# Attention scores of two heads issued together on alternating row halves, and a gating stage with 512-column mixing matmuls

## Chip, core and metric

One core of a Trainium2 chip runs one launch. The metric is the device time of that launch in microseconds (us). The kernel before takes 1171.48 us (median of three runs, 1170.75 to 1171.59).

## What is computed

The reference runs two layers on a (256, 2048) fp32 activation. Layer 0 normalises the rows, projects to queries, keys, values and gates, runs two banded attention mixers of 16 heads of width 64 each, gates both with SiLU, projects back and adds the residual. Layer 1 normalises, projects to u, v and a gate, and mixes v over positions:

```python
s = einsum('bgrnqd,bgnkd->bgrnqk', qb, kb) + bias[:, :, None]   # scores, both mixers
p = exp(s - m[..., None]);  u = einsum('bgrnqk,bgnkd->bgrnqd', p, vb)
...
v = _rms(v, v_g).reshape(Bn, S // 128, 128, 16, 256)            # layer 1
ws = w_s * tril(ones)                                           # 16 groups of 128x128
s = einsum('gts,bnsgc->bntgc', ws, v) + b_s.T[:, :, None]
y = u * s.reshape(Bn, S, 4096) * gate;  return x + y @ w_out
```

So a head has a 128 x 256 score block (the second 128 queries against all 256 keys) and a 128 x 128 block (the first 128 queries), and layer 1 mixes 256 columns of v per group, once per chunk n of 128 positions (two chunks).

## The kernel before, in words

**Projections.** `gemm` (lines 100 to 126) makes a 256 x 512 output block from weights that stream in through SP's DMA queue. `wtile` (lines 75 to 88) splits each 256 x 512 weight tile into a rounded part `whi` (ScalarE, line 85) and a rest `wlo` (VectorE, line 86), and three fp32r matmuls of 512 columns each (lines 121 to 123) add up the product. There are 44 such calls with 512 columns (the last block of the last one is cut into halves) and one with 256.

**Fillers.** After every second bank-and-k step, that is after six matmuls of 512 columns, `gemm` calls `fill()` (line 92), which advances the oldest generator of a list by one `yield`. Attention, gating, transposes and splits are such generators; so their instructions are written between the matmuls of the next projection. The tile framework then orders each engine's instructions by this order and by its own estimate of when operands and buffers are free, so that neighbours can change places.

**Attention** (lines 275 to 368) is called four times with eight heads. Step i of the loop (line 359) issues `scores(i)`, `ptrans(i-3)` and `pv(i-5)`, then yields; the `tiny`, `sb`, `pr` and `pt` tiles come from pools (`mid`: 10 buffers for `sb`, `pr`, `pt`). `scores(i)` (line 282) takes one of two "s" PSUM banks and issues, on row half i % 2 (partitions 0 to 63 or 64 to 127, where the 64 values of the head lie), three fp32r matmuls of 256 columns (lines 296 to 298) and one fp32 matmul of 128 columns (line 299), which the engine runs as two. VectorE adds the bias and takes maxima (lines 302, 305, 310 or 313), ScalarE the exponentials (lines 315, 317). `ptrans` (line 321) transposes the three 128 x 128 blocks into the one "t" bank and ScalarE copies them out (line 327); `pv` (line 332) multiplies them by v, 64 columns each (lines 339 to 341, two passes each).

**Gating** (lines 547 to 604). `ws` holds the masked mixing matrices. `sgu(c)`, eight times, scales the two matrices of its groups by the row norm of v on GpSimd (`wsn`, line 577), once per chunk n, splits them (`wsh` line 579, `wsl` line 580), splits v (`vh` line 582, `vl` line 583), and issues, per chunk and group, three matmuls of 256 columns (lines 589 to 591), then adds the bias and multiplies by u on VectorE (line 594). After that it waits for the gate, multiplies on GpSimd (line 601) and transposes (line 377). The row norm `rsv` (line 567) is known after the last of eight v projections.

Of the kernel before, what the change touches and what calls it, by code (L numbers as in the profile page):

```python
# [10 lines left out]
F32 = mybir.dt.float32  # L11
# [22 lines left out]
def trunk(ctx, tc, x, xT, ev_g, w_in0, w_kva, qk_g, sinks, w_out0, od_g, w_in1, v_g, w_sT, b_s,  # L34
# [2 lines left out]

    cons = ctx.enter_context(tc.tile_pool(name="cons", bufs=1))
    wpool = ctx.enter_context(tc.tile_pool(name="wpool", bufs=4))
    big = ctx.enter_context(tc.tile_pool(name="big", bufs=26))  # L40
    mid = ctx.enter_context(tc.tile_pool(name="mid", bufs=10))
    tiny = ctx.enter_context(tc.tile_pool(name="tiny", bufs=4))
    ps = ctx.enter_context(tc.tile_pool(name="ps", bufs=4, space=bass.MemoryType.PSUM))

# [12 lines left out]
    def psum(tag, bufs):  # L57
        return ps.tile([P, 512], F32, tag=tag, bufs=bufs, name=nm(tag))
# [216 lines left out]
    def attention(mix, h0, first_bias, qTb, kTb, vfn, ydst):  # L275

        (q0, q1), (k0, kh, kl) = qTb, kTb
        bts = [first_bias, None]
        st = {}
        grp = {}  # L280

        def scores(i):
            h = h0 + i
            if i % 4 == 0:
                bt = bts[i // 4]
                nmx = tiny.tile([P, 4, 2], F32, tag="nmx", name=nm("nmx"))
                mx = tiny.tile([P, 4, 2], F32, tag="mx", name=nm("mx"))
                l = tiny.tile([P, 4, 2], F32, tag="l", name=nm("l"))
                grp[i // 4] = (bt, mx, nmx, l)
            bt, mx, nmx, l = grp[i // 4]  # L290
            j = i % 4
            half = slice((i % 2) * 64, (i % 2) * 64 + 64)
            sp = psum("s", 2)
            kp = h // 8 if mix == 0 else i // 2
            qh, ql = q1[half, 0, i // 2, :], q1[half, 1, i // 2, :]
            nc.tensor.matmul(sp[:, 0:256], qh, kh[half, kp, :], start=True, stop=False)  # L296
            nc.tensor.matmul(sp[:, 0:256], qh, kl[half, kp, :], start=False, stop=False)
            nc.tensor.matmul(sp[:, 0:256], ql, kh[half, kp, :], start=False, stop=True)
            nc.tensor.matmul(sp[:, 256:384], q0[half, i // 2, :], k0[half, kp, :],  # L299
                             start=True, stop=True)  # L300
            sb = m2([P, 384], nm("sb"))
            nc.vector.tensor_tensor_reduce(out=sb[:, 0:256], in0=sp[:, 0:256], in1=bt[:, j, :],  # L302
                                           scale=1.0, scalar=NEG, op0=ALU.add, op1=ALU.max,
                                           accum_out=mx[:, j, 1:2])
            nc.vector.tensor_tensor_reduce(out=sb[:, 256:384], in0=sp[:, 256:384],
                                           in1=bt[:, j, P:2 * P],
                                           scale=1.0, scalar=NEG, op0=ALU.add, op1=ALU.max,
                                           accum_out=mx[:, j, 0:1])
            if mix == 0:
                nc.vector.tensor_scalar(nmx[:, j, :], mx[:, j, :], snk[:, h:h + 1], -1.0,  # L310
                                        op0=ALU.max, op1=ALU.mult)
            else:
                nc.vector.tensor_scalar(nmx[:, j, :], mx[:, j, :], -1.0, None, op0=ALU.mult)  # L313
            pr = m2([P, 384], nm("pr"))
            nc.scalar.activation(pr[:, 0:256], sb[:, 0:256], AF.Exp, bias=nmx[:, j, 1:2],  # L315
                                 accum_out=l[:, j, 1:2])
            nc.scalar.activation(pr[:, 256:384], sb[:, 256:384], AF.Exp, bias=nmx[:, j, 0:1],
                                 accum_out=l[:, j, 0:1])
            st[i] = pr

        def ptrans(i):
            pr = st[i]
            tp = psum("t", 1)
            for b in range(3):
                nc.tensor.transpose(tp[:, b * P:(b + 1) * P], pr[:, b * P:(b + 1) * P], ident)  # L325
            pt = m2([P, 384], nm("pt"))
            nc.scalar.copy(pt, tp[:, 0:384])
            st[i] = pt

        ub = {}  # L330

        def pv(i):
            pt = st.pop(i)
            if i % 4 == 0:
                ub[0] = psum("u", 1)
            up = ub[0].rearrange("p (t h d) -> p t h d", t=2, d=DH)
            j = i % 4
            v0, v1 = vfn(i)
            nc.tensor.matmul(up[:, 0, j, :], pt[:, 256:384], v0, start=True, stop=True)  # L339
            nc.tensor.matmul(up[:, 1, j, :], pt[:, 0:128], v0, start=True, stop=False)  # L340
            nc.tensor.matmul(up[:, 1, j, :], pt[:, 128:256], v1, start=False, stop=True)  # L341
            if j == 3:
                _, mx, nmx, l = grp[i // 4]
                if mix == 0:
                    es = tiny.tile([P, 4, 2], F32, tag="es", name=nm("es"))
                    hh = h0 + i - 3
                    nc.vector.tensor_tensor(es, nmx,
                                            snk[:, hh:hh + 4].unsqueeze(2).broadcast_to([P, 4, 2]),
                                            op=ALU.add)
                    nc.scalar.activation(es, es, AF.Exp)  # L350
                    nc.vector.tensor_tensor(l, l, es, op=ALU.add)
                r = tiny.tile([P, 4, 2], F32, tag="rl", name=nm("rl"))
                nc.vector.reciprocal(r, l)
                yv = ydst.rearrange("p t (h d) -> p t h d", d=DH)[:, :, i - 3:i + 1, :]
                nc.vector.tensor_tensor(yv, up,
                                        r.rearrange("p h t -> p t h").unsqueeze(3)
                                        .broadcast_to([P, 2, 4, DH]), op=ALU.mult)

        for i in range(8 + L2):
            if i < 8:  # L360
                scores(i)
            if L1 <= i < 8 + L1:
                ptrans(i - L1)
            if i >= L2:
                pv(i - L2)
            if i == 0:
                bts[1] = bias_tile(mix, h0 + 4)
            yield

    def split_T(y, yT, q, tags):  # L370
# [173 lines left out]
    nc.scalar.dma_start(trit, tri)  # L544
    bst = cons.tile([P, 16], F32, name="bst")
    nc.scalar.dma_start(bst, b_s)
    ws = []
    for j in range(2):
        t = c4([P, 8, P], nm("ws"))
        nc.gpsimd.dma_start(t, w_sT[j].rearrange("s (g t) -> s g t", g=8))  # L550
        nc.gpsimd.tensor_tensor(t, t, trit.unsqueeze(1).broadcast_to([P, 8, P]), op=ALU.mult)
        ws.append(t)

    in1 = lambda c: gemm(yTk(hT1), KT, w_in1[c], 512)
    ssv = cons.tile([P, 2, 8], F32, name="ssv")
# [14 lines left out]

    def sgu(c, u, gate):
        y = c4([P, 2, 512], nm("y"))
        wsn = m2([P, 2, 2, P], nm("wsn"))
        wsh = mid.tile([P, 2, 2, P], F32R, tag="m2", name=nm("wsh"))
        wsl = mid.tile([P, 2, 2, P], F32R, tag="m2", name=nm("wsl"))
        for n in range(2):
            nc.gpsimd.tensor_scalar(wsn[:, n], ws[c // 4][:, (2 * c) % 8:(2 * c) % 8 + 2, :],  # L577
                                    rsv[:, n:n + 1], None, op0=ALU.mult)
        nc.scalar.copy(wsh, wsn)
        nc.vector.tensor_tensor(wsl, wsn, wsh.bitcast(F32), op=ALU.subtract)  # L580
        vh, vl = c4([P, 2, 512], nm("vh"), F32R), c4([P, 2, 512], nm("vl"), F32R)
        nc.scalar.copy(vh, vt[c])  # L582
        nc.vector.tensor_tensor(vl, vt[c], vh.bitcast(F32), op=ALU.subtract)  # L583
        yield
        for n in range(2):
            sp = psum("s", 2)
            for gi in range(2):
                cs = slice(gi * 256, (gi + 1) * 256)
                nc.tensor.matmul(sp[:, cs], wsh[:, n, gi, :], vh[:, n, cs], start=True, stop=False)
                nc.tensor.matmul(sp[:, cs], wsh[:, n, gi, :], vl[:, n, cs], start=False, stop=False)  # L590
                nc.tensor.matmul(sp[:, cs], wsl[:, n, gi, :], vh[:, n, cs], start=False, stop=True)  # L591
            for gi in range(2):
                cs = slice(gi * 256, (gi + 1) * 256)
                nc.vector.scalar_tensor_tensor(y[:, n, cs], sp[:, cs],
                                               bst[:, 2 * c + gi:2 * c + gi + 1], u[:, n, cs],
                                               op0=ALU.add, op1=ALU.mult)
            yield
        while gate[0] is None:
            yield
        yield  # L600
        nc.gpsimd.tensor_tensor(y, y, gate[0], op=ALU.mult)  # L601
        yield
        yield
        yield from split_T(y, yT1, c, [("t", 1), ("u", 1)])
# [85 lines left out]
```

## Time and profile before

| what | value |
| --- | --- |
| median of three runs | 1171.48 us (1170.75 to 1171.59) |
| profiled execution, its own time | 1171.01 us |
| its span, first to last instruction of the program | 1169.2 us |
| TensorE matmuls (PE) | 1162.0 us busy, 99% of the span |
| TensorE weight loads (PEld) | 963.0 us, 82% |
| VectorE (DVE) / ScalarE (ACT) / GpSimd (POOL) | 55% / 51% / 12% |

The profiled time lies 1.8 us above its span, and 0.5 us under the median. A matmul's busy time includes the latency of the array and overlaps the next one's, so what a matmul costs in a stream is read from the distance of the starts, not from its duration.

### The profile page before, as it was taken

What the parts mean: (1) busy time and instruction counts of PE and PEld (TensorE: products, weight loads), DVE (VectorE), ACT (ScalarE), POOL (GpSimd) and SP (SyncE); (2) the same over time, 40 slices, a digit from 0 to 9 for tenths busy, and PEclk for the clock granted to TensorE, in tenths of its full rate; (3) what the DMA queues carried; (4) which work ended last, traced back from release to release, by engine and by line L of the source; (5) the groups of instructions that cost most, each with busy time, mean ns of one, the idle gap of its engine ahead of it and who ended that gap; (6) DMA issues with size and microseconds to landing.
All of it is one profiled execution on the core that took longest, in us unless ns stands there. A gap on an engine that the chain in (4) does not pass through costs nothing.

```text
span 1169.2 us, 14610 instructions
## 1 busy us (share of the span) xinstructions
PE 1162.0 (99%) x5546; PEld 963.0 (82%) x5546; DVE 647.5 (55%) x837; ACT 595.2 (51%) x818; POOL 135.7 (12%) x85
## 2 busy tenths in 40 slices
PE   9999999999999999999999999999999999999998
PEld 7887888788788888888888888888888888888887
DVE  6586556655645555554556555565556555454453
ACT  6556654544654544544545554555464455433332
POOL 0131111112103000211215110100000000000000
PEclk9999999999999999999999999999999999999999
DMA  9675335436436655666665555555555665566661
GB/s 349 232 245 195 127 108 184 172 109 208 160 123 219 196 186 183 203 212 200 202 213 178 184 188 190 181 178 187 186 187 171 190 187 173 198 215 199 200 213 37
DMA packets 63638, 218.37 MB, mean 187 GB/s; under 512 B 7632, under 2 KB 10320, under 8 KB 63312
## 3 DMA queue, kind: packets, MB, share of 16 engines
q1 hardware_dynamic: 60352, 209.74, 55.3%
q0 software_dynamic: 2080, 7.34, 2.0%
q8 instruction: 43, 0.70, 0.2%
q10 hardware_dynamic: 1136, 0.36, 0.1%
q14 instruction: 27, 0.22, 0.1%
HBM read 215.32 MB, written 2.10 MB: 186 GB/s over the span
## 4 chain that ended last, share of the span: by engine, by line
PE 96%; DVE 1%; POOL 1%; ACT 1%; DMA 0%; issue 0%; SPq 0%; ACTq 0%; POOLq 0%
PE g L121 30%; PE g L123 29%; PE g L122 29%; PE t L325 1%; POOL wsn L577 1%; PE s L296 1%; PE t L377 1%; PE s L299 1%; PE u L340 1%; PE u L341 1%; PE t L218 1%; PE u L339 1%; DVE wlo L86 0%; DMA wraw<-in_w_in_dram 0%; ACT whi L85 0%
## 5 line engine op out<-in xcount | busy, mean ns | idle before, releaser
L86 DVE TENSOR_TENSOR wlo<-wraw,whi 128x1024 fp32r<-128x1024 f32 (+1 forms) x393 | 514.0, 1312 | 427.3 <-ACT whi L85 426.5
L85 ACT CAST whi<-wraw 128x1024 fp32r<-128x1024 f32 (+1 forms) x393 | 409.1, 1043 | 480.9 <-PE g L123 457.1
L121 PE MATMUL g<-whi,hTh 128*128 128x512 f32 (+1 forms) x1184 | 464.6, 393 | 0.6 <-ACT whi L85 0.6
L122 PE MATMUL g<-wlo,hTh 128*128 128x512 f32 (+1 forms) x1184 | 458.9, 388 | 0.5 <-DVE wlo L86 0.5
L123 PE MATMUL g<-whi,hTl 128*128 128x512 f32 (+1 forms) x1184 | 459.4, 388 | 0.0
L121 PEld LDWEIGHTS g<-whi,hTh 128*128 128x128 f32 x1184 | 222.4, 188 | 45.2 <-ACT whi L85 1.0
L123 PEld LDWEIGHTS g<-whi,hTl 128*128 128x128 f32 x1184 | 222.5, 188 | 44.7
L122 PEld LDWEIGHTS g<-wlo,hTh 128*128 128x128 f32 x1184 | 222.7, 188 | 42.5 <-DVE wlo L86 1.0
L121 PE MATMUL g<-whi,yTh 128*128 128x512 f32 (+1 forms) x416 | 156.2, 375 | 0.0
L122 PE MATMUL g<-wlo,yTh 128*128 128x512 f32 (+1 forms) x416 | 155.3, 373 | 0.0
L123 PE MATMUL g<-whi,yTl 128*128 128x512 f32 (+1 forms) x416 | 155.2, 373 | 0.0
L123 PEld LDWEIGHTS g<-whi,yTl 128*128 128x128 f32 x416 | 78.3, 188 | 14.1
L122 PEld LDWEIGHTS g<-wlo,yTh 128*128 128x128 f32 x416 | 78.4, 188 | 13.5
L121 PEld LDWEIGHTS g<-whi,yTh 128*128 128x128 f32 x416 | 78.4, 188 | 13.6
L601 POOL TENSOR_TENSOR y<-y,gt 128x1024 f32<-128x1024 f32 x8 | 19.2, 2405 | 265.2 <-ACT gt L191 265.2
L565 POOL TENSOR_TENSOR v<-v,gv 128x1024 f32<-128x1024 f32 x8 | 21.9, 2743 | 220.2 <-ACT junk L562 220.2
L302 DVE CUSTOM_DVE_ANT_0 sb<-s,bias 128x256 f32<-128x256 f32 x32 | 13.5, 422 | 27.7 <-PE s L299 27.7
L577 POOL TENSOR_SCALAR wsn<-ws,rstdv 128x256 f32<-128x256 f32 x16 | 20.3, 1282 | 60.6 <-PE s L591 57.3
L191 ACT ACT_TABLE_LOAD x20 | 25.7, 1283 | 1.0 <-PE g L123 0.7
L315 ACT ACTIVATE pr<-sb,nmx 128x256 f32<-128x256 f32 x32 | 16.3, 510 | 18.9 <-DVE nmx L313 13.6
L272 POOL TENSOR_TENSOR bias<-bias,ba 128x1024 f32<-128x1024 f32 x8 | 20.8, 2598 | 33.9 <-DMA bias<-in_bias_dram 33.9
L583 DVE TENSOR_TENSOR vl<-v,vh 128x1024 fp32r<-128x1024 f32 x8 | 9.8, 1225 | 16.4 <-ACT vh L582 16.4
(130 smaller groups left out, 627.3 us busy)
## 6 DMA issues: line engine op xcount, KB each, us to landing
wraw<-in_w_in_dram SPq DMA_DIRECT2D x287, 512.0 KB, 3.7
wraw<-in_w_out_dram SPq DMA_DIRECT2D x96, 512.0 KB, 3.6
bias<-in_bias_dram POOLq DMA_DIRECT2D x8, 512.0 KB, 3.9
xT<-in_xT_dram SPq DMA_DIRECT2D x8, 256.0 KB, 5.1
xr<-in_x_dram SPq DMA_DIRECT2D x2, 1024.0 KB, 10.9
wraw<-in_w_kva_dram SPq DMA_DIRECT2D x8, 256.0 KB, 3.4
gv<-in_v_g_dram POOLq DMA_DIRECT2D x8, 256.0 KB, 3.1
out_dram<-o SPq DMA_DIRECT2D x7, 256.0 KB, 5.0
```

What stands on the lines that cost most here:

```text
L85: nc.scalar.copy(hi[:, js, :cw], raw[:, js, :cw])
L86: nc.vector.tensor_tensor(lo[:, js, :cw], raw[:, js, :cw], hi[:, js, :cw].bitcast(F32), op=ALU.subtract)
L121: nc.tensor.matmul(o, ah[:, sl], whi[:, k, a:b], start=st, stop=False)
L122: nc.tensor.matmul(o, ah[:, sl], wlo[:, k, a:b], start=False, stop=False)
L123: nc.tensor.matmul(o, al[:, sl], whi[:, k, a:b], start=False, stop=en)
L191: nc.scalar.activation(z[:, tt, :cw], acc[tt][:, :cw], func, scale=rs[:, tt:tt + 1])
L272: nc.gpsimd.tensor_tensor(bt, bt, ba[:, mix:mix + 1, :].broadcast_to([P, 4, 256]), op=ALU.add)
L302: nc.vector.tensor_tensor_reduce(out=sb[:, 0:256], in0=sp[:, 0:256], in1=bt[:, j, :], scale=1.0, scalar=NEG, op0=ALU.add, op1=ALU.max, acc ...
L315: nc.scalar.activation(pr[:, 0:256], sb[:, 0:256], AF.Exp, bias=nmx[:, j, 1:2], accum_out=l[:, j, 1:2])
L565: nc.gpsimd.tensor_tensor(v, v, gv.unsqueeze(1).broadcast_to([P, 2, 512]), op=ALU.mult)
L577: nc.gpsimd.tensor_scalar(wsn[:, n], ws[c // 4][:, (2 * c) % 8:(2 * c) % 8 + 2, :], rsv[:, n:n + 1], None, op0=ALU.mult)
L601: nc.gpsimd.tensor_tensor(y, y, gate[0], op=ALU.mult)
```

## The change

`scores` now takes an even head number and issues two heads at once, into two "s" banks: the three fp32r matmuls in the order first head, second head, first head, and so on, then the two fp32 matmuls. The loop goes in steps of two with two yields each: first the two score blocks, then two `ptrans` and two `pv` after the next yield (14 yields for 13). In the gating stage the masked matrices are split once, ahead of the stage; the row norm goes into the split of v (ScalarE with a scale per row, VectorE multiply and subtract, per chunk); and the mixing matmuls run per group over both chunks, 512 columns each. The buffers are 27 for the large pool (26 before) and 9 for `mid` (10).

```diff
-    big = ctx.enter_context(tc.tile_pool(name="big", bufs=26))
-    mid = ctx.enter_context(tc.tile_pool(name="mid", bufs=10))
+    big = ctx.enter_context(tc.tile_pool(name="big", bufs=27))
+    mid = ctx.enter_context(tc.tile_pool(name="mid", bufs=9))
...
-            sp = psum("s", 2)
-            kp = h // 8 if mix == 0 else i // 2
-            qh, ql = q1[half, 0, i // 2, :], q1[half, 1, i // 2, :]
-            nc.tensor.matmul(sp[:, 0:256], qh, kh[half, kp, :], start=True, stop=False)
-            nc.tensor.matmul(sp[:, 0:256], qh, kl[half, kp, :], start=False, stop=False)
-            nc.tensor.matmul(sp[:, 0:256], ql, kh[half, kp, :], start=False, stop=True)
-            nc.tensor.matmul(sp[:, 256:384], q0[half, i // 2, :], k0[half, kp, :],
-                             start=True, stop=True)
...
+            sps = [psum("s", 2), psum("s", 2)]
+            halves = [slice(0, 64), slice(64, 128)]
+            for qpart, kpart, st_, en_ in ((0, kh, True, False), (0, kl, False, False),
+                                           (1, kh, False, True)):
+                for sp, half in zip(sps, halves):
+                    nc.tensor.matmul(sp[:, 0:256], q1[half, qpart, pq, :], kpart[half, kp, :],
+                                     start=st_, stop=en_)
+            for sp, half in zip(sps, halves):
+                nc.tensor.matmul(sp[:, 256:384], q0[half, pq, :], k0[half, kp, :],
+                                 start=True, stop=True)
+            for i, sp in zip((i0, i0 + 1), sps):
...
-        for i in range(8 + L2):
+        for i in range(0, 8 + L2 + 1, 2):
             if i < 8:
                 scores(i)
-            if L1 <= i < 8 + L1:
-                ptrans(i - L1)
-            if i >= L2:
-                pv(i - L2)
-            if i == 0:
-                bts[1] = bias_tile(mix, h0 + 4)
+                if i == 0:
+                    bts[1] = bias_tile(mix, h0 + 4)
+            yield
+            for k in (i, i + 1):
+                if L1 <= k < 8 + L1:
+                    ptrans(k - L1)
+                if L2 <= k < 8 + L2:
+                    pv(k - L2)
             yield
...
         nc.gpsimd.tensor_tensor(t, t, trit.unsqueeze(1).broadcast_to([P, 8, P]), op=ALU.mult)
-        ws.append(t)
+        wsh, wsl = c4([P, 8, P], nm("wsh"), F32R), c4([P, 8, P], nm("wsl"), F32R)
+        nc.scalar.copy(wsh, t)
+        nc.vector.tensor_tensor(wsl, t, wsh.bitcast(F32), op=ALU.subtract)
+        ws.append((wsh, wsl))
...
         for n in range(2):
-            nc.gpsimd.tensor_scalar(wsn[:, n], ws[c // 4][:, (2 * c) % 8:(2 * c) % 8 + 2, :],
-                                    rsv[:, n:n + 1], None, op0=ALU.mult)
-        nc.scalar.copy(wsh, wsn)
-        nc.vector.tensor_tensor(wsl, wsn, wsh.bitcast(F32), op=ALU.subtract)
-        vh, vl = c4([P, 2, 512], nm("vh"), F32R), c4([P, 2, 512], nm("vl"), F32R)
-        nc.scalar.copy(vh, vt[c])
-        nc.vector.tensor_tensor(vl, vt[c], vh.bitcast(F32), op=ALU.subtract)
+            nc.scalar.activation(vh[:, n, :], vt[c][:, n, :], AF.Copy, scale=rsv[:, n:n + 1])
+            nc.vector.scalar_tensor_tensor(vl[:, n, :], vt[c][:, n, :], rsv[:, n:n + 1],
+                                           vh[:, n, :].bitcast(F32),
+                                           op0=ALU.mult, op1=ALU.subtract)
...
-        for n in range(2):
+        for gi in range(2):
             sp = psum("s", 2)
...
+            nc.tensor.matmul(o, wsh[:, g, :], vh[:, :, cs], start=True, stop=False)
+            nc.tensor.matmul(o, wsh[:, g, :], vl[:, :, cs], start=False, stop=False)
+            nc.tensor.matmul(o, wsl[:, g, :], vh[:, :, cs], start=False, stop=True)
+            nc.vector.scalar_tensor_tensor(y[:, :, cs], o, bst[:, 2 * c + gi:2 * c + gi + 1],
+                                           u[:, :, cs], op0=ALU.add, op1=ALU.mult)
```

## Rows read from the trace of the kernel before

**Rows 1.** The page: busy time by engine, granted clock in 40 slices, the chain.

```profile
PE 1162.0 (99%) x5546; PEld 963.0 (82%) x5546; DVE 647.5 (55%) x837; ACT 595.2 (51%) x818; POOL 135.7 (12%) x85
...
PEclk9999999999999999999999999999999999999999
...
PE 96%; DVE 1%; POOL 1%; ACT 1%; DMA 0%; issue 0%; SPq 0%; ACTq 0%; POOLq 0%
```

**Rows 2.** Timeline, 98.8 to 101.2 us: start, duration (us), engine, line, operation.

```profile
98.92 0.39 PE L122 MATMUL g<-wlo,hTh 128*128 128x512 f32 x1
...
99.15 0.39 PE L123 MATMUL g<-whi,hTl 128*128 128x512 f32 x1
99.46 0.18 PEld L296 LDWEIGHTS s<-kh,q 64*128 64x128 f32 x1 [0.35 <-issue]
99.46 0.38 PE L296 MATMUL s<-kh,q 64*128 64x256 f32 x1
99.57 0.19 PEld L297 LDWEIGHTS s<-kl,q 64*128 64x128 f32 x1
...
99.69 0.28 PE L297 MATMUL s<-kl,q 64*128 64x256 f32 x1
...
99.80 0.28 PE L298 MATMUL s<-kh,q 64*128 64x256 f32 x1
...
99.92 0.38 PE L299 MATMUL s<-k,q 64*128 64x128 f32 x2
...
100.23 0.50 PE L121 MATMUL g<-whi,hTh 128*128 128x512 f32 x1
...
100.57 0.40 PE L122 MATMUL g<-wlo,hTh 128*128 128x512 f32 x1
```

**Rows 3.** By line and form, whole span: busy us, mean ns, idle before, releaser.

```profile
L577 POOL TENSOR_SCALAR wsn<-ws,rstdv 128x256 f32<-128x256 f32 x16 | 20.3, 1282 | 60.6 <-PE s L591 57.3 <-DVE rstdv L184 3.4
...
L327 ACT COPY pt<-t 128x384 f32<-128x384 f32 x32 | 14.9, 467 | 7.7 <-PE t L325 7.7
...
L302 DVE CUSTOM_DVE_ANT_0 sb<-s,bias 128x256 f32<-128x256 f32 x32 | 13.5, 422 | 27.7 <-PE s L299 27.7
...
L296 PE MATMUL s<-kh,q 64*128 64x256 f32 x32 | 12.2, 382 | 0.0
L299 PE MATMUL s<-k,q 64*128 64x128 f32 x64 | 12.2, 270 | 0.0
...
L583 DVE TENSOR_TENSOR vl<-v,vh 128x1024 fp32r<-128x1024 f32 x8 | 9.8, 1225 | 16.4 <-ACT vh L582 16.4
...
L589 PE MATMUL s<-vh,wsh 128*128 128x256 f32 x32 | 8.9, 279 | 0.0
```

**Rows 4.** Timeline of PE, 121 to 134 us: one head's transposes and pv.

```profile
122.89 0.49 PE L325 MATMUL t<-ident,pr 128*128 128x128 f32 x3
...
123.39 0.39 PE L340 MATMUL u<-kva,pt 128*128 128x64 f32 x2
123.61 0.39 PE L341 MATMUL u<-kva,pt 128*128 128x64 f32 x2
123.81 0.48 PE L123 MATMUL g<-whi,hTl 128*128 128x512 f32 x1
```

**Rows 5.** Timeline of PE, 693 to 699 us: mixing matmuls, then projection matmuls.

```profile
694.76 0.28 PE L589 MATMUL s<-vh,wsh 128*128 128x256 f32 x1
...
695.48 0.40 PE L121 MATMUL g<-whi,hTh 128*128 128x512 f32 x1
...
696.41 0.39 PE L122 MATMUL g<-wlo,hTh 128*128 128x512 f32 x1
...
697.77 0.39 PE L122 MATMUL g<-wlo,hTh 128*128 128x512 f32 x1
```

**Rows 6.** Stretches (first attention, gating): busy us of each engine, clock, DMA share.

```profile
99.00:133.00 34.00, 34.00 (x191) 27.23 (x189) 17.29 (x56) 26.18 (x57) 0.00 (x0) 1.00 0.34 105
...
650.00:990.00 340.00, 340.00 (x1567) 282.94 (x1566) 184.71 (x174) 176.55 (x188) 25.07 (x13) 1.00 0.58 184
```

More of the change, by code (lines that the diff above doesn't have):

```diff
@@ L280, in attention, with scores @@
         grp = {}
[L282 to L285, printed above, removed]
+        def scores(i0):
+            if i0 % 4 == 0:
                 nmx = tiny.tile([P, 4, 2], F32, tag="nmx", name=nm("nmx"))
@@ L288, in scores @@
                 l = tiny.tile([P, 4, 2], F32, tag="l", name=nm("l"))
[L289 to L292, printed above, removed]
-            sp = psum("s", 2)
-            kp = h // 8 if mix == 0 else i // 2
-            qh, ql = q1[half, 0, i // 2, :], q1[half, 1, i // 2, :]
-            nc.tensor.matmul(sp[:, 0:256], qh, kh[half, kp, :], start=True, stop=False)
-            nc.tensor.matmul(sp[:, 0:256], qh, kl[half, kp, :], start=False, stop=False)
@@ L298, in scores @@
-            nc.tensor.matmul(sp[:, 0:256], ql, kh[half, kp, :], start=False, stop=True)
-            nc.tensor.matmul(sp[:, 256:384], q0[half, i // 2, :], k0[half, kp, :],
-                             start=True, stop=True)
[L301 to L319, printed above, removed]
+                grp[i0 // 4] = (bts[i0 // 4], mx, nmx, l)
+            bt, mx, nmx, l = grp[i0 // 4]
+            pq = i0 // 2
+            kp = (h0 + i0) // 8 if mix == 0 else pq
@@ new lines, in scores @@
+            for i, sp in zip((i0, i0 + 1), sps):
+                h = h0 + i
+                j = i % 4
+                sb = m2([P, 384], nm("sb"))
+                nc.vector.tensor_tensor_reduce(out=sb[:, 0:256], in0=sp[:, 0:256],
+                                               in1=bt[:, j, :],
+                                               scale=1.0, scalar=NEG, op0=ALU.add, op1=ALU.max,
+                                               accum_out=mx[:, j, 1:2])
+                nc.vector.tensor_tensor_reduce(out=sb[:, 256:384], in0=sp[:, 256:384],
+                                               in1=bt[:, j, P:2 * P],
+                                               scale=1.0, scalar=NEG, op0=ALU.add, op1=ALU.max,
+                                               accum_out=mx[:, j, 0:1])
+                if mix == 0:
+                    nc.vector.tensor_scalar(nmx[:, j, :], mx[:, j, :], snk[:, h:h + 1], -1.0,
+                                            op0=ALU.max, op1=ALU.mult)
+                else:
+                    nc.vector.tensor_scalar(nmx[:, j, :], mx[:, j, :], -1.0, None, op0=ALU.mult)
+                pr = m2([P, 384], nm("pr"))
+                nc.scalar.activation(pr[:, 0:256], sb[:, 0:256], AF.Exp, bias=nmx[:, j, 1:2],
+                                     accum_out=l[:, j, 1:2])
+                nc.scalar.activation(pr[:, 256:384], sb[:, 256:384], AF.Exp,
+                                     bias=nmx[:, j, 0:1], accum_out=l[:, j, 0:1])
+                st[i] = pr
@@ L572, in sgu @@
         y = c4([P, 2, 512], nm("y"))
-        wsn = m2([P, 2, 2, P], nm("wsn"))
-        wsh = mid.tile([P, 2, 2, P], F32R, tag="m2", name=nm("wsh"))
-        wsl = mid.tile([P, 2, 2, P], F32R, tag="m2", name=nm("wsl"))
+        vh, vl = c4([P, 2, 512], nm("vh"), F32R), c4([P, 2, 512], nm("vl"), F32R)
         for n in range(2):
-            nc.gpsimd.tensor_scalar(wsn[:, n], ws[c // 4][:, (2 * c) % 8:(2 * c) % 8 + 2, :],
-                                    rsv[:, n:n + 1], None, op0=ALU.mult)
@@ L584, in sgu @@
+        wsh, wsl = ws[c // 4]
         yield
-        for n in range(2):
+        for gi in range(2):
             sp = psum("s", 2)
[L587 to L596, printed above, removed]
+            o = sp.rearrange("p (n c) -> p n c", n=2)
+            cs = slice(gi * 256, (gi + 1) * 256)
+            g = (2 * c + gi) % 8
+            nc.tensor.matmul(o, wsh[:, g, :], vh[:, :, cs], start=True, stop=False)
[3 more added lines that the diff above has]
+                                           u[:, :, cs], op0=ALU.add, op1=ALU.mult)
```

## Prediction

> **What bounds the kernel now.** I read the page first: matmuls cover 99% of the span, the granted clock is full in every slice (2.4 GHz, the upper of the two levels), and 96% of the chain that ended last is PE [rows 1]. So PE's stream of matmuls is the bound, and a part of the change is worth what it takes out of that stream, or puts in. A matmul's printed duration includes latency, so the stream is read from start to start in a timeline. Next, the timeline around one score burst [rows 2]: projection matmuls of 512 columns follow each other after 0.23 us (98.92 to 99.15). The first score matmul starts 0.31 after the last of them, 0.08 late; its weight load starts with it, not ahead of it, so the next one comes 0.23 later (99.46 to 99.69) instead of about 0.115, which is what the two behind it need (99.69, 99.80, 99.92). The same toll is paid on the way out: 99.92 to 100.23 for two fp32 passes, and 0.34 instead of 0.23 for the first projection matmul behind. There is one such burst per head, 32 in all, with 64 fp32 passes (L296, L299 [rows 3]). In the other stages I looked at the stretches: in the first attention ScalarE is busy 26.18 of 34 us and VectorE 17.29, in the gating stage 176.55 and 184.71 of 340 [rows 6]; both have room, and GpSimd has more.
>
> **Price of a burst.** From L123 at 99.15 to the second projection matmul at 100.57 are 1.42 us; two projection distances (0.46) lie in it anyway, so a burst costs 0.96 [rows 2]. The streaming in it is 3 x 0.115 for the 256-column matmuls and 2 x 0.11 for the fp32 passes, 0.565 (the passes' 0.11 is taken from L340 to L341, 0.22 for two passes [rows 4]). The other 0.395, some 0.40, is the toll for changing from 128 to 64 rows and back.
>
> **Scores, the toll.** 16 bursts of two heads instead of 32 of one: 16 x 0.395 = 6.3 us less. Nothing hides this: it lies in PE's stream.
>
> **Scores, the alternation.** No row of before shows matmuls on different row halves next to each other, because projections stand between any two heads. So its price is bounded from both sides. (a) In turn: each still takes 0.115; a pair costs 0.395 + 2 x 0.565 = 1.53, against 1.92 for two bursts. (b) Side by side: the second head's matmul runs with the first's. The three steps take 3 x 0.115; of the fp32 passes (order: first head twice, then second head twice) only one finds a partner, if matmuls start in program order, so 3 x 0.11. A pair then costs 0.395 + 0.345 + 0.33 = 1.07 and saves 0.85, or 13.6 us for 16. (c) Each change of half pays the entry toll of [rows 2], 0.08 late start and 0.115 exposed weight load: seven changes in a pair, 7 x 0.195 = 1.37 more.
> I take (b). The rows for it: two operands, two row halves and two PSUM banks have nothing in common but the issue; a weight load already runs beside the streaming matmul of its own half (L297's load at 99.57 under L296 [rows 2]), and the toll comes where the shape of the used rows changes, which it does not between halves. The row against it: where matmuls are short, loads pace the stream. 64 columns take as long as 128, two passes in 0.22 [rows 4], so if two halves cannot be loaded at once, (a) holds, because a score matmul then has a load of the same length in front of it.
> The Trainium skill, TensorEngine Tiling (Array Packing), Key Properties, says that different tiles can load weights and multiply in parallel, and that changing the tiling mode, not just the tile, drains the engine. By it (b) holds and the sum is the forecast; by the pacing of loads in rows 4 alone it would be (a), 7 us more. No row here shows the first half of the rule; the toll in rows 2 agrees with the second.
>
> **Transposes and pv in twos.** A head's transposes and pv take 122.89 to 123.81, 0.92 us, whether one follows another or not [rows 4]. New is that the second head's transposes want the single "t" bank again as soon as the first's are copied out: 0.47 us on ScalarE (L327 [rows 3]). In program order a pv of 0.92 - 0.33 = 0.59 us (three transposes of 0.11 subtracted) stands between and covers the copy, unless ScalarE is late; projection matmuls can cover it too. If that cover is gone, 12 such places (three per attention call) cost up to 0.5 each, 6 us. I take 0.5 in all. A few bursts before went straight into transposes and saved part of the exit toll; that is inside this 0.5.
>
> **Softmax for two heads in one burst.** VectorE now gets two score blocks at once; per head its first pass takes 0.42 (L302 [rows 3]) and the whole some 1.1 us. The next pair is due two fills, at least 12 projection matmuls or 2.7 us plus the pair itself, later, so the banks come free in time: cost nothing, up to 1 us a pair if projections' splits delay VectorE. One yield more per call moves pv back one fill; the result of the last call is read a projection later, so nothing waits. One `mid` buffer less holds (nine live at most): the same cover.
>
> **Gating.** Twelve matmuls of 256 columns become six of 512. Six of the former take 694.76 to 695.48, 0.72; six of the latter 696.41 to 697.77, 1.36 [rows 5]. So 1.44 becomes 1.36, eight times: 0.6 us less. GpSimd loses 16 scalings, 20.3 us (L577 [rows 3]), none of which PE waited for; its queue holds the multiplication by the gate behind them, with idle time to spare. ScalarE and VectorE lose eight conversions of 512 columns each and gain two of 1024 each ahead of the stage, at most 1.23 each by L583 [rows 3]; the split of v goes by chunk, with the row norm in it, a few tenths more per call on each engine, beside 340 - 185 us of free VectorE time [rows 6]. At the first call the split waits for the row norm, as the scaled matrices did; a stall of some tenths either way. Two more large tiles stay live with one buffer more; at the last call one half of v's split may have to wait for a projection operand to come free, with a projection of 22 us (96 x 0.23) as cover. No DMA is added or moved; SP's queue is as before. Cost: nothing.
>
> **Sum.** -13.6 + 0.5 - 0.6 = -13.7 us. Against the profiled execution's 1171.0 us that is 1157.3; the median lies 0.5 above that execution, so 1157.8.
>
> **The rivals.**
> *In turn* (a): the halves take turns, since loads pace them. -6.3 + 0.5 - 0.6 = -6.4, so 1165.1. For it: rows 4; against it: separate rows, and the load that already runs beside a matmul.
> *Drain at each change of half* (c), the slower side: 16 x (1.37 - 0.395) = +15.6, with the rest +15.5, so 1187.0. It decides when a change costs more than 0.06 us (0.40 over seven changes): above that the kernel is slower. For it: the toll exists in rows 2; against it: there the number of rows changes, here only their place.
> *The order undone*: the second bank is not free when the framework orders PE's work, so a pair is cut in two with projections between, and the second transposes wait. Then the tolls come back and up to 6 us are added: 1166 to 1177, about 1171. For it: the order follows estimates, and two "s" banks leave no spare; against: the two fills of room above.
>
> **Chances.** Measurement of this kernel tells some 0.2% (2.3 us) from no change. Side by side 0.45, in turn 0.34, drain 0.09, order undone 0.12. The first two are both faster by over 0.2%, and 0.03 of the last: 0.82. Same: 0.06, all of the order undone. Slower: drain 0.09 and 0.03 of the last, 0.12. The range takes in side by side with its unknowns (a fourth fp32 pass hidden as well, -1.8 us, and 1 us of stalls less than taken) and in turn with 2.5 us of its own: 1155.2 to 1167.5.
>
> **What the profile after should show.** Score matmuls of two heads within a few hundredths of each other, then a step of about 0.12, a pair taking 1.07 us beyond two projection distances: side by side. Even steps of 0.115, the pair 1.53: in turn. Steps of 0.2 to 0.3 within a burst: drain. More than 16 bursts, or projections inside one: the order undone. Mixing matmuls 0.23 apart, no `wsn` on GpSimd, and idle PE in front of transposes if the copy is late. The forecast is wrong if the first distance is not there, whatever the tolls do.

## The result, and the profile after

The changed kernel takes 1158.97 us (median of four runs, 1158.16 to 1159.27) against 1171.24 us for the kernel before on the same chip: a ratio of 0.9894, 95% interval 0.9881 to 0.9906, 12.3 us less. The forecast was 1157.8 us, from 1155.2 to 1167.5. In a second set of runs, beside other executions of the kernel before, the ratio was again 0.9894 (0.9877 to 0.9910).

The page of the changed kernel, parts 1, 2 and 4, against [rows 1]:

```profile
span 1157.1 us, 14468 instructions
...
PE 1149.3 (99%) x5498; PEld 952.8 (82%) x5498; DVE 641.3 (55%) x823; ACT 592.7 (51%) x820; POOL 115.5 (10%) x69
...
PEclk9999999999999999999999999999999999999999
...
PE 95%; DVE 1%; ACT 1%; DMA 1%; issue 1%; SPq 0%; ACTq 0%
```

TensorE is still the bound, at full granted clock. There are 48 matmuls fewer, the mixing matmuls of double width, and GpSimd is 20 us less busy. The span fell by 12.1 us.

The timeline of the first burst, with the columns of [rows 2]:

```profile
99.41 0.39 PE L123 MATMUL g<-whi,hTl 128*128 128x512 f32 x1
99.73 0.19 PEld L298 LDWEIGHTS s<-kh,q 64*128 64x128 f32 x2 [0.35 <-issue]
99.73 0.38 PE L298 MATMUL s<-kh,q 64*128 64x256 f32 x2
...
99.95 0.28 PE L298 MATMUL s<-kl,q 64*128 64x256 f32 x2
...
100.07 0.28 PE L298 MATMUL s<-kh,q 64*128 64x256 f32 x2
...
100.19 0.38 PE L301 MATMUL s<-k,q 64*128 64x128 f32 x4
...
100.50 0.50 PE L121 MATMUL g<-whi,hTh 128*128 128x512 f32 x1
...
100.83 0.40 PE L122 MATMUL g<-wlo,hTh 128*128 128x512 f32 x1
```

Each score line now stands for two matmuls (x2), or four passes (x4), and takes no longer than it did for one: two matmuls take 0.38 us from first start to last end, with a step of 0.12 to the next two, and the four fp32 passes take the 0.31 that two took. Weight loads come in pairs too. From L123 at 99.41 to L122 at 100.83 are 1.42 us, exactly the 1.42 of one head in [rows 2]. Two heads for the price of one.

I added up, over all matmuls of the span, the distance from each start to the next start. It gives the stream by kind, before and after: scores 24.8 and 14.4 us, mixing 11.9 and 11.0, the 4512 projection matmuls of 512 columns with what stands behind them 1042.8 and 1041.9, transposes 26.5 and 26.7, pv 19.4 and 19.2. The differences add up to -12.2 us; the span's is -12.1.

Not every burst is clean. Of 16 pairs, 12 cost 0.97 to 0.99 us, priced as in the prediction. Timeline of PE, one that waits for its second bank (103.44), one that was cut in two (from 113.25), one with transposes inside (from 229.64):

```profile
103.44 0.38 PE L298 MATMUL s<-kh,q 64*128 64x256 f32 x1
104.13 0.38 PE L298 MATMUL s<-kh,q 64*128 64x256 f32 x1 [0.30 <-DVE mx L311]
...
113.25 0.38 PE L298 MATMUL s<-kh,q 64*128 64x256 f32 x1
...
114.03 0.50 PE L121 MATMUL g<-whi,hTh 128*128 128x512 f32 x1
114.46 0.38 PE L298 MATMUL s<-kh,q 64*128 64x256 f32 x1
...
229.99 0.28 PE L298 MATMUL s<-kh,q 64*128 64x256 f32 x2
230.28 0.55 PE L331 MATMUL t<-ident,pr 128*128 128x128 f32 x3
230.76 0.49 PE L301 MATMUL s<-k,q 64*128 64x128 f32 x4
```

In the first, the second head's matmul stands 0.69 behind the first head's, until VectorE has emptied its bank (`mx`, line 311). The second has one projection matmul between its heads and pays the toll twice: the two halves cost 1.08 each. A like place to the third is at 309.84; each pays a second toll around its transposes. The breaks in the second and third stand in the program itself, in the order that the framework wrote; the first is a wait on the chip. And there are two new halts ahead of transposes, 1.34 us at 136.0 and 0.79 at 187.3 (counted as the distance of two starts beyond the usual 0.23), where one of 1.20 at 212.9 in the kernel before has shrunk to 0.40. The timeline around the larger:

```profile
133.07 2.40 POOL L400 TENSOR_TENSOR ya<-ya,gt 128x1024 f32<-128x1024 f32 x1 [33.87 <-DVE ya L361]
...
134.09 2.46 DVE L86 TENSOR_TENSOR wlo<-wraw,whi 128x1024 fp32r<-128x1024 f32 x1 [1.14 <-ACT whi L85]
...
136.47 0.47 DVE L231 SCALAR_TENSOR_TENSOR q<-t,gain,q 128x256 fp32r<-128x256 f32 x1
...
137.04 0.47 ACT L234 ACTIVATE q<-t,gain 128x256 f32<-128x256 f32 x1 [2.62 <-DVE q L231]
...
137.57 0.66 PE L218 MATMUL t<-ident,qa 128*128 128x128 f32 x4 [1.18 <-ACT q L234]
```

The transposes of the next queries want the "t" bank; ScalarE's last read of it waits for VectorE's, and that stands behind a split of weights that took 2.46 us, twice the usual. It started while GpSimd multiplied by the gate (133.07 to 135.47) and ended 1.08 us after the product.

### The profile page after: what moved, and what is told of

It reads as the page before. It is cut to its first block, busy times and chain, and to the rows that moved or that the text cites. A ratio compares the mean times of both kernels' runs of the same rounds, so it can differ in the third digit from the quotient of the medians.

```text
span 1157.1 us, 14468 instructions
## 1 busy us (share of the span) xinstructions
PE 1149.3 (99%) x5498; PEld 952.8 (82%) x5498; DVE 641.3 (55%) x823; ACT 592.7 (51%) x820; POOL 115.5 (10%) x69
## 4 chain that ended last, share of the span: by engine, by line
PE 95%; DVE 1%; ACT 1%; DMA 1%; issue 1%; SPq 0%; ACTq 0%
PE g L121 30%; PE g L122 30%; PE g L123 30%; PE t L331 1%; DMA wraw<-in_w_in_dram 1%; ACT whi L85 1%; DVE wlo L86 1%; PE s L298 1%; PE u L347 1%; PE u L346 1%; PE t L385 1%; PE u L345 0%; PE t L218 0%; PE s L599 0%; PE s L600 0%
## 5 line engine op out<-in xcount | busy, mean ns | idle before, releaser
L122 PE MATMUL g<-wlo,hTh 128*128 128x512 f32 (+1 forms) x1184 | 459.5, 388 | 0.6 <-DVE wlo L86 0.6
L123 PE MATMUL g<-whi,hTl 128*128 128x512 f32 (+1 forms) x1184 | 458.9, 388 | 0.0
L123 PEld LDWEIGHTS g<-whi,hTl 128*128 128x128 f32 x1184 | 222.6, 188 | 45.0
L122 PEld LDWEIGHTS g<-wlo,hTh 128*128 128x128 f32 x1184 | 222.8, 188 | 44.0 <-DVE wlo L86 1.4
L122 PE MATMUL g<-wlo,yTh 128*128 128x512 f32 (+1 forms) x416 | 155.3, 373 | 0.0
L123 PE MATMUL g<-whi,yTl 128*128 128x512 f32 (+1 forms) x416 | 155.3, 373 | 0.0
L123 PEld LDWEIGHTS g<-whi,yTl 128*128 128x128 f32 x416 | 78.3, 188 | 14.1
L121 PEld LDWEIGHTS g<-whi,yTh 128*128 128x128 f32 x416 | 78.4, 188 | 13.6
L122 PEld LDWEIGHTS g<-wlo,yTh 128*128 128x128 f32 x416 | 78.4, 189 | 13.5
L608 POOL TENSOR_TENSOR y<-y,gt 128x1024 f32<-128x1024 f32 x8 | 19.2, 2404 | 344.9 <-ACT gt L191 344.9
L577 POOL TENSOR_TENSOR v<-v,gv 128x1024 f32<-128x1024 f32 x8 | 22.1, 2757 | 219.5 <-ACT junk L574 219.5
L333 ACT COPY pt<-t 128x384 f32<-128x384 f32 x32 | 15.0, 469 | 9.8 <-PE t L331 9.8
L588 DVE SCALAR_TENSOR_TENSOR vl<-v,rstdv,vh 128x512 fp32r<-128x512 f32 x16 | 11.3, 749 | 12.4 <-ACT vh L587 12.4
```

What stands on the lines that cost most here:

```text
L121: nc.tensor.matmul(o, ah[:, sl], whi[:, k, a:b], start=st, stop=False)
L122: nc.tensor.matmul(o, ah[:, sl], wlo[:, k, a:b], start=False, stop=False)
L123: nc.tensor.matmul(o, al[:, sl], whi[:, k, a:b], start=False, stop=en)
L577: nc.gpsimd.tensor_tensor(v, v, gv.unsqueeze(1).broadcast_to([P, 2, 512]), op=ALU.mult)
```

## The experiments

Each ratio is to the kernel before, measured with the same set of runs (its medians there: 1172.31, 1172.01 and 1172.36 us for the three sets).

**Both heads on one row half.**

```diff
-            halves = [slice(0, 64), slice(64, 128)]
+            halves = [slice(0, 64), slice(0, 64)]
```

> The changed kernel with both heads of a pair read from row half 0 (so every odd head computes the scores of the even head; that part of the result is another one). Order, banks, counts and tolls stay. Theory (halves run side by side): without the second half a burst costs 0.40 of toll and ten steps of 0.11 to 0.12, 1.53 us instead of 0.97; 16 bursts give +9.0 us, so 1168 us. Rival (the gain comes from halving the bursts and from alternating banks alone): stays at 1159 us, with bursts of 0.97 us.

Measured: 1166.23 us, ratio 0.9947 (0.9932 to 0.9962), so 6.2 us more than the changed kernel by the ratios. Timeline of PE, the first burst:

```profile
99.93 0.50 PE L298 MATMUL s<-kh,q 64*128 64x256 f32 x2
100.27 0.39 PE L298 MATMUL s<-kl,q 64*128 64x256 f32 x2
100.50 0.40 PE L298 MATMUL s<-kh,q 64*128 64x256 f32 x2
100.73 0.60 PE L301 MATMUL s<-k,q 64*128 64x128 f32 x4
101.27 0.50 PE L121 MATMUL g<-whi,hTh 128*128 128x512 f32 x1
```

Two matmuls now take 0.23 where the pair took 0.12, and four passes 0.54 instead of 0.31; the burst costs 1.55. So the second row half is what runs beside; banks and bunching alone give the rest. This kernel is the case "in turn" of the prediction, with 1.53 worked out for a burst. That it lies 6.2 us below the kernel before, where 6.4 was worked out, is closer than it can be known: the interval goes from 4.5 to 8.0, and the profiled executions of the two kernels are 3.3 apart. The profiled execution took 1167.7, as expected, with a span 8.8 us above the changed kernel's; the scores make 7.7 of them (14.4 to 22.1 us), less than 9.0 because two of the changed kernel's bursts were cut or halted anyway, and a new halt in front of transposes at 295 us makes 1.5. The other executions are 0.7 to 2.4 us shorter, so the median misses the expectation by 1.8.

**First head, then second head, in one burst.**

```diff
-            for qpart, kpart, st_, en_ in (...):
-                for sp, half in zip(sps, halves):
-                    nc.tensor.matmul(sp[:, 0:256], ...)
-            for sp, half in zip(sps, halves):
-                nc.tensor.matmul(sp[:, 256:384], ...)
+            for sp, half in zip(sps, halves):
+                for qpart, kpart, st_, en_ in (...):
+                    nc.tensor.matmul(sp[:, 0:256], ...)
+                nc.tensor.matmul(sp[:, 256:384], ...)
```

> The changed kernel with the same pairs in one burst, but all four matmuls of the first head ahead of all four of the second. Theory (only neighbours on different halves run side by side, and matmuls start in program order): at most one step of ten is shared, where the first head's last pass meets the second head's first matmul; bursts of 1.42 to 1.53 us, 16 x 0.45 to 0.56 = +7 to +9 us, so 1166 to 1168 us. Rival (the engine itself finds the partner further back in its queue): 1159 us.

Measured: 1164.13 us, ratio 0.9930 (0.9916 to 0.9943): 4.2 us more than the changed kernel, half of what the theory wanted. Timeline of PE, the first burst (line 300 is the fp32 matmul here; in the program's order, also as the framework wrote it, both passes of the first head's line 300 stand ahead of the second head's line 298):

```profile
99.54 0.38 PE L298 MATMUL s<-kh,q 64*128 64x256 f32 x1
99.76 0.28 PE L298 MATMUL s<-kl,q 64*128 64x256 f32 x1
99.77 0.39 PE L298 MATMUL s<-kh,q 64*128 64x256 f32 x2
99.99 0.28 PE L298 MATMUL s<-kl,q 64*128 64x256 f32 x1
99.99 0.38 PE L300 MATMUL s<-k,q 64*128 64x128 f32 x2
100.11 0.28 PE L298 MATMUL s<-kh,q 64*128 64x256 f32 x1
100.22 0.38 PE L300 MATMUL s<-k,q 64*128 64x128 f32 x2
100.53 0.50 PE L121 MATMUL g<-whi,hTh 128*128 128x512 f32 x1
```

Five matmuls of line 298 have started before the first pass of line 300, and only three of them can be the first head's. So the engine starts the second head's matmuls ahead of earlier ones on the other half. It finds the partner from the second step on, not from the first; a burst costs 1.20, between 0.97 and 1.53. Both the theory (order is kept) and the rival (order is of no matter) fall: the order in the program is worth 0.23 us a burst (16 of them 3.7 of the 4.2 us), and three fifths of the overlap (1.55 to 1.20 of 1.55 to 0.97) come without it.

**One part of the change alone.** The gating part on the kernel before, and the attention part with the gating of before (both with the new pool sizes).

> The kernel before with the gating change alone (matrices split once, norm on v's split, 512-column mixing matmuls, pools of 27 and 9). Theory: the mixing matmuls go from 11.9 to 11.0 us of PE's stream, and nothing else moves: -0.6 to -0.9 us, 1170.4 us. Rival (the gating part carries more, through the 20 us of GpSimd work it removes): 1168 us or less.

> The changed kernel with the gating stage of before (pools of 27 and 9 kept). Theory: the attention part carries -11.4 us: 1159.9 us, bursts of 0.97 us as in the changed kernel. Rival (the two parts need each other): clearly above 1161 us.

Measured: gating alone 0.9989 (0.9978 to 0.9999), attention alone 0.9898 (0.9882 to 0.9914). Page, part 1, of gating alone, then of attention alone:

```profile
PE 1161.3 (99%) x5498; PEld 960.6 (82%) x5498; DVE 644.5 (55%) x823; ACT 594.2 (51%) x820; POOL 114.8 (10%) x69
```

```profile
PE 1149.8 (99%) x5546; PEld 954.4 (82%) x5546; DVE 647.6 (56%) x837; ACT 593.2 (51%) x818; POOL 136.0 (12%) x85
```

PE's busy time falls by 0.7 and by 12.2 us against [rows 1]. Attention carries the result. For gating the time's interval holds both -0.6 and -0.9 us and cannot tell them apart; the stream can: mixing matmuls from 11.9 to 11.0 us. The 20 us taken from GpSimd gave nothing that the time shows.

**More room between pairs.** The bursts' losses and the halts made about 4 us; the five kernels from here on ask whether they can be had back. First a further yield behind the scores; then one behind each head's transposes.

```diff
                 if i == 0:
                     bts[1] = bias_tile(mix, h0 + 4)
+                yield
             yield
```

> The changed kernel with one more yield between a pair's scores and the transposes, for the first four steps of a call, so that pairs stand three fills apart instead of two. Theory (what the bursts lost comes from VectorE not having emptied the second bank): no burst is cut or halted, some 1.9 us less in PE's stream of scores (14.4 to 12.5 us) and 1157 us. Rival (the cuts come from transposes becoming ready in the middle of a burst, whatever the distance): bursts with transposes inside stay, 1159 us.

```diff
                     pv(k - L2)
-            yield
+                yield
```

> The changed kernel with a yield after each head's transposes and pv instead of after two of them, so that pairs stand three fills apart and the two transposes of a step have a fill between them. Theory: as with the extra yield no burst is cut for its bank, and the transposes' waits for the single t bank go too (0.5 us in all by the trace of the changed kernel): 1156.5 us. Rival (later pv and later gates push waits into the k and q transposes and the splits): 1159 us or more.

Measured: 0.9915 (0.9900 to 0.9929) and 0.9917 (0.9902 to 0.9932), some 2.5 us slower than the changed kernel. Who waited for whom, PE alone, of the extra yield (total us, times, longest):

```profile
PE t L386 <- DVE yTl L391: 2.7, 1, 2.7
PE t L218 <- ACT k L248: 2.6, 2, 1.4
...
PE s L298 <- DVE mx L311: 0.6, 1, 0.6
```

With the extra yield no pair is cut in two, but one still halts for its bank, two still have transposes inside (1.6 and 2.0 us without these), the scores stay at 14.6 us, and the halts ahead of transposes are longer: the theory failed. With a yield behind each head it failed too: two pairs halt for a bank and cost 1.83 and 2.02 us, two are broken up by other work, and the longest wait for the "t" bank is 1.3 us. The waits move with the places of the yields, and these places were worse.

**Work moved from GpSimd to VectorE.** First the gate multiplications alone, then the bias additions too, then the head norms' products as well.

```diff
-        nc.gpsimd.tensor_tensor(y, y, gate, op=ALU.mult)
+        nc.vector.tensor_tensor(y, y, gate, op=ALU.mult)
...
-        nc.gpsimd.tensor_tensor(bt, bt, ba[:, mix:mix + 1, :].broadcast_to([P, 4, 256]), op=ALU.add)
+        nc.vector.tensor_tensor(bt, bt, ba[:, mix:mix + 1, :].broadcast_to([P, 4, 256]), op=ALU.add)
```

> The changed kernel with the four multiplications of the attention output by its gate on VectorE instead of GpSimd. Theory (the halt of 1.3 us in front of the q transposes at 136 us comes from a split of weights that takes 2.46 instead of 1.23 us while GpSimd multiplies): no split beside a gate multiplication is longer than 1.3 us, the halt at 136 us is gone, -1 us: 1158 us. Rival (the halt comes from ScalarE's or the t bank's order): the halt stays, 1159 us or more.

> The changed kernel with the eight bias additions and the four gate multiplications of the attention stage on VectorE instead of GpSimd. Theory (the halts left in the changed kernel come from VectorE work that takes twice as long while GpSimd works on a tile of 1024 columns): a bias addition takes 1.2 us on VectorE instead of 2.6 on GpSimd and no longer stretches a split; the halt at 136 us and the one in the second burst go, 2 to 3 us less, 1157 us. Rival (VectorE's longer queue halts TensorE elsewhere): 1159 us or more.

> As bias_and_gate_on_vector, and the squares and scalings of the head norms on VectorE too, so that GpSimd does no arithmetic between the projections of layer 0. Theory: no split of weights beside an attention call is longer than 1.3 us, and the time is 1157 us or a little less. Rival: 12 operations of 1.2 us more in VectorE's queue ahead of the q and k transposes bring new halts, 1159 us or more.

Measured: 0.9889 (0.9872 to 0.9905), 0.9885 (0.9868 to 0.9901) and 0.9915 (0.9901 to 0.9930). With the gate on VectorE the halt at the same place is gone; the timeline there:

```profile
136.30 1.23 DVE L400 TENSOR_TENSOR ya<-ya,gt 128x1024 f32<-128x1024 f32 x1
...
137.45 1.22 DVE L86 TENSOR_TENSOR wlo<-wraw,whi 128x1024 fp32r<-128x1024 f32 x1
...
138.58 0.48 DVE L231 SCALAR_TENSOR_TENSOR q<-t,gain,q 128x256 fp32r<-128x256 f32 x1
...
139.78 0.60 PE L218 MATMUL t<-ident,qa 128*128 128x128 f32 x4
```

The product takes 1.23 us on VectorE and the split behind it its usual 1.22; the transposes start without idle time. The time did not follow: 1159.76 us, against 1159.72 of the changed kernel in the same set. Its profiled execution, at 1161.83 us the longest of the four, shows a larger halt in the second burst instead, 2.12 us for the bank, and the clock behind it. Timeline of PE, then the stretch behind it (columns as in [rows 6]):

```profile
105.86 0.38 PE L298 MATMUL s<-kh,q 64*128 64x256 f32 x1 [2.12 <-DVE mx L311]
...
107.15 0.63 PE L122 MATMUL g<-wlo,hTh 128*128 128x512 f32 x1
107.57 0.63 PE L123 MATMUL g<-whi,hTl 128*128 128x512 f32 x1
```

```profile
106.00:111.00 5.00, 5.00 (x23) 4.02 (x24) 3.03 (x13) 2.99 (x11) 0.00 (x0) 0.66 0.15 34
```

Behind that idle time the projection matmuls stand 0.42 apart instead of 0.23, the lower level of 1.2 GHz; the mean granted clock of the 5 us is 0.66. This halt cost more than itself. What kept the other three executions, 1159.17 to 1159.88 us, from gaining the microsecond no trace shows.

With the bias additions on VectorE too, the profiled span is 1155.4 us, the shortest here, against 1157.2 for the changed kernel's in the second set: the halts at 136 and 212 us and the one in the second burst are absent, and so is one at 293 us that the changed kernel's second trace has. PE's waits there, from the who-waited-for-whom view:

```profile
PE t L136 <- DVE wz L131: 1.1, 1, 1.1
PE t L385 <- DVE yTl L390: 0.6, 1, 0.6
PE g L121 <- ACT whi L85: 0.5, 1, 0.5
PE g L122 <- DVE wlo L86: 0.5, 1, 0.5
PE t L331 <- ACT pt L333: 0.2, 1, 0.2
```

Only one wait for a k, q or y transpose is left. But the ratio's interval lies across that of the changed kernel, so 1.8 us of one profiled execution is all that stands for a gain, and the times do not settle it. With the norms on VectorE as well the time is the rival's, but its mechanism, new halts ahead of the q and k transposes, is not in the trace: there are none. The profiled execution has 3.1 us of waits for `whi`, but these end at 8.62 and 12.65 us, ahead of any head norm, where ScalarE itself waits for weights to land. New behind them is 1.67 us at the last y transposes, where the masks of the mixing matrices still run on GpSimd. Why the other executions, 1162.66 to 1164.08 us, are longer stays open:

```profile
7.95 0.62 ACT L85 CAST whi<-wraw 128x512 fp32r<-128x512 f32 x1 [2.60 <-DMA wraw<-in_w_in_dram]
...
334.29 2.39 POOL L560 TENSOR_TENSOR ws<-ws,trit 128x1024 f32<-128x1024 f32 x1 [3.37 <-DMA ws<-in_w_sT_dram]
...
334.66 3.11 DVE L86 TENSOR_TENSOR wlo<-wraw,whi 128x1024 fp32r<-128x1024 f32 x1 [1.49 <-ACT whi L85]
...
338.42 0.66 PE L385 MATMUL t<-ident,yb 128*128 128x128 f32 x4 [1.67 <-DVE yTl L390]
```

## Why the prediction was right

**The bound and the price of a burst** held: every microsecond of the gain is in PE's stream of starts, 12.2 of it, and a clean burst costs what the rows of one head said.

**Alternation.** The choice of (b) among three bounds was right and is shown: pairs start 0.003 us apart in the trace, and on one half a burst costs 1.55 where 1.53 was worked out for (a). The time alone did not show it, since the range took in (a) too, at 1165.1. Drain (c) is excluded by the same pairs. What I called the row against it, loads that pace short matmuls, does not reach across the halves: two loads run at once on two halves. Whether it is the loads that set the 0.11 to 0.12 on one half was not tested. The Trainium skill's statement in TensorEngine Tiling (Array Packing), Key Properties, that tiles load and multiply in parallel, agrees with these pairs.

**A term too small: the fp32 passes.** "If matmuls start in program order" cost me 0.11 us a burst. The passes start in pairs 0.003 us apart, as two on one half never do (0.11), so first head and second head run side by side in both, and a burst is 0.97 and not 1.07; 16 clean ones would have saved 15.3 us instead of 13.6. The range allowed for this, as the fourth pass hidden; the sum did not. The Trainium skill, TensorE: Matmul & The Clock Gate, Part 3, has matmuls strictly first in, first out; in the run with the heads one behind the other, matmuls of the other row half start ahead of earlier ones (five of line 298 before the first of line 300), and the measurement decides.

**A term put at nothing: softmax for two heads.** "Cost nothing, up to 1 us a pair" was the step that failed. One pair waited for its second bank, 0.69 us more than a clean pair, and one was cut in two, 1.2 us more; two more had transposes inside, 0.45 each, 2.8 us in all. Only the first is shown to wait for VectorE; the other three, 2.1 us, are the rival "order undone" on a small scale, which the sum put at nothing too. So the scores gave 12.5 (30.9 us of bursts before, 18.4 after, transposes not counted) where 13.6 stood. The two errors partly cancel, and that the median came within 1.2 us of the forecast is in part luck.

**Transposes in twos** were put at 0.5; the two waits for the "t" bank at 110.2 and 155.3 took 0.24 and 0.32; the kernel before had one of 0.30 at 164.5. **Gating**, put at -0.6, came to -0.9 in its stream; about half a microsecond is the doubled width, the rest the halt of the first call, 0.59 between two starts at 646.2, that is no longer there. **Not in the sum** were the halts ahead of transposes, +1.3 us net (1.34 + 0.79 - 0.80). So: -12.5 for the scores, -0.9 for gating, +1.3 for these halts and +0.3 for the "t" bank make -11.8, within 0.3 of the span's -12.1, against -13.7. (Waits for the first weights, up to 13 us, are 0.2 shorter than in the kernel before.)

Where those last halts come from is shown for the one at 136 us (it goes with the gate's product). That they could be had back for good is not: of the kernels that removed it one brought a longer halt elsewhere, one a halt at the last y transposes, and the gain of the third, 1.8 us of one execution, lies inside the intervals.

## What to carry to other kernels

Two matmuls of 64 rows cost one here, next to each other on the two row halves and into different banks (one bank for both was not tried). Interleave them step by step, and gather as many as banks allow (more than two heads were not tried), because the change from 128 to 64 rows and back costs 0.4 us. Leave room for the engine that empties the banks: a pair needs both at once, a late bank halted one for 0.69 us, and a pair that is cut pays the toll again, 1.2 us more in all. Where TensorE is 99% busy, price a change by distances between starts, kind by kind, and keep a term for halts that only move.

## What was not expected of the hardware

Matmuls on different row halves do not keep the program's order: five of line 298 started before the first of line 300 in the run with one head behind the other. The two passes of neighbouring fp32 matmuls interleave, four passes in 0.31 us. And a VectorE operation with two operands of 1024 columns, 1.23 us by itself, took 2.46 and 3.11 us beside a GpSimd product of the same size; moved off GpSimd, that product took 1.23 instead of 2.40 and the split behind it 1.22. The split is not slowed throughout but held: in the changed kernel's trace all 33 splits of this size that start while GpSimd multiplies or adds on 1024 columns end 1.08 or 1.09 us after it, at whatever point of it they start, and the 16 that are under way when it starts keep their 1.22 to 1.23. So what counts is which of the two starts first.
